# A two-layer hybrid encoder on one core: psE over strips, float32 attention, stores on GpSimd's queue, four raw buffers, and down products added to the residual in DRAM by accumulating DMAs

## The chip, the cores and the metric

One core of one Trainium2 chip runs the whole program in one launch. The metric is device time in microseconds (us); lower is better. The measured programs take the same inputs and lay the same arrays out in DRAM. Engines are named as the profile names them: PE is the matrix engine, with PEld its weight loads; DVE the vector engine, ACT the scalar engine, POOL the GpSimd engine, SP the engine whose queue issues DMAs.

## The reference

Two pre-norm residual layers over 1024 tokens of width 1024, everything in float32:

```
for layer in range(2):
    hn = rmsnorm(h, norm1_g); proj = hn @ w_in          # u 512, q 512, k 128, v 128, two gates of 1024
    y_a = s5_branch(u)      # 32 groups x 64 complex states, both directions, then gelu and a GLU
    y_b = windowed_gqa(q, k, v)   # 8 query heads, 2 key heads, width 64, window +-128, sink, relative bias
    merged = sigmoid(gate_a) * (y_a @ w_branch_a) + sigmoid(gate_b) * (y_b @ w_branch_b)
    h = h + merged @ w_out
    hn2 = rmsnorm(h, norm2_g)
    h = h + (silu(hn2 @ w_gate) * (hn2 @ w_up)) @ w_down    # inner width 2816
return rmsnorm(h, final_g)
```

Attention works on blocks of 128 queries against up to three blocks of 128 keys.

## The kernel before

Activations are kept transposed: a tile is 128 channels by 512 tokens (`HC`), and `h` runs over the two token halves. A float32 product is made of three `fp32r` products. `split` writes a rounded copy (`hi`, on ACT) and the remainder (`lo`, on DVE), and `chain` issues hi·hi, hi·lo and lo·hi for each of the k tiles of 128, so that a product over 1024 channels is 24 matmuls of 128x512. In the feed-forward part most pairs of gate and up columns are done as a `Quad`: seven products of four k tiles each (`qx`, `qy`, `qv`, `qw`) in place of eight.

Weights come in granules of up to 128x1024. `fetch` loads a granule into a `raw` buffer over SP's queue, `parts` or `quad_part` splits it (`whi` on ACT, `wlo` on DVE). There are two raw buffers and three pairs of split buffers, and `ahead` loads one granule beyond the one that is split.

The work is a list of items in a fixed order (`self.seq`), made by mixing lists by hand: projections are laid between the pieces of the state-space preparation (`s5_prep_pair`), of attention (`attention_items`) and of the state-space branch (`s5_items`). `emit` goes through the list and issues each item's instructions to the engines' queues, each of which works in order. Nearly all small tiles come from one pool `A` of `N_SLOTS` = 90 slots of 128x512 float32; PSUM has eight banks (`PS`). Every DMA, loads and stores, is issued on SP's queue (`nc.sync`).

The parts that the change touches:

- `s5_prep_pair` runs for 16 pairs of groups in each layer (layer 0: mixed with its first projections; layer 1: mixed with layer 0's feed-forward part). Its last step transposes `WB` (`pswb`) and makes, for this pair, eight small float32 products into 32 rows of `psE`: four with 112 columns (L642) and four with 16 (L644). After four pairs the bank is copied out.
- Attention: for each key head and block, `att_scores` makes for each of four heads two fp32r products over 128 rows that hold the hi and the lo part of a 64-wide query (`qe`, `qo`), with the keys' `kh` and `kl`; L793 adds the bias and takes the row maximum on DVE, ACT takes the exponential, `att_scale` divides (L810). `att_transpose` turns the probabilities and splits them (`ph`, `pl`), and `att_values` multiplies both with a value tile that holds hi and lo side by side, and adds the two halves on ACT and DVE (L832, L842).
- The state-space branch: `s5_load` reads five arrays for a pair from DRAM on SP's queue, `s5_states` makes 8 products into the two 64-row halves of a bank (`s5x`) and scans them on DVE, `s5_output` makes 12 float32 products (`s5y`), `s5_store` writes the result (`zd`).
- The feed-forward part works through groups of inner tiles (`GROUPS`). After a group's gate and up products come 16 `down` items, one for each (m, h): for a group of n tiles 3n matmuls into `dn`. Before, each item reads the residual tile from `hs` in DRAM (three items ahead), adds `dn` on DVE (L1210) and stores it back (L1212). The last group's results are kept and feed the next norm.

## Time and profile before

| | us |
|---|---|
| median of 3 runs | 2750.16 (2749.1 to 2753.0) |
| the profiled execution | 2751.03 |
| its span in the profile | 2749.2 |

Mean granted clock of PE in the profiled execution: 0.983 of full speed. The profile divides the span by engine and instruction. A busy PE is one with a matmul in flight; matmuls overlap, so what PE takes for one in a stream is read from the distance of starts in the timeline and not from the duration of one.

### The profile page before, as it was taken

The numbers are of one execution on the slowest core, as the hardware profiler recorded it, in microseconds if no ns is written. First come the engines' busy times: TensorE is split into PE (matmuls) and PEld (weight loads), VectorE is DVE, ScalarE is ACT, GpSimd is POOL, SyncE is SP. The second block draws the span as 40 slices with busy tenths as digits, with TensorE's granted clock in tenths as the row PEclk, the third lists the DMA queues.
The fourth block names the chain that finished last, engine by engine and source line by source line (L and its number), as shares of the span: only waits on it lengthen the run. The fifth ranks groups of instructions, "written<-read, shape, count | busy, mean of one in ns | idle before, by whom it ended". The sixth has DMA issues, their size and how long they took to land.

```text
span 2749.2 us, 35031 instructions
## 1 busy us (share of the span) xinstructions
PE 2651.0 (96%) x12738; PEld 2182.3 (79%) x12738; DVE 1880.3 (68%) x3881; ACT 972.1 (35%) x1829; POOL 0.2 (0%) x4
## 2 busy tenths in 40 slices
PE   8999997899999999999999999999999999999996
PEld 6788876688788888888878888888877888878775
DVE  8977988674965666656675877756377566656656
ACT  5325754432322222222345653343233223212222
POOL 0000000000000000000000000000000000000000
PEclk9999998999999999999999999999999999999998
DMA  3453235354245342553342135534415433543453
GB/s 118 133 164 112 95 113 172 120 202 139 84 125 187 105 147 73 176 169 106 123 167 75 56 108 177 177 122 154 134 65 176 162 103 131 180 161 94 138 173 132
DMA packets 205053, 367.47 MB, mean 134 GB/s; under 512 B 22304, under 2 KB 70688, under 8 KB 204880
## 3 DMA queue, kind: packets, MB, share of 16 engines
q1 hardware_dynamic: 204880, 365.23, 40.4%
q8 instruction: 100, 1.64, 0.2%
q14 instruction: 73, 0.60, 0.1%
HBM read 246.70 MB, written 118.44 MB: 133 GB/s over the span
## 4 chain that ended last, share of the span: by engine, by line
PE 80%; DVE 11%; DMA 5%; ACT 2%; issue 2%; SPq 1%; DVEq 0%; ACTq 0%
PE pj L174 6%; PE pj L175 6%; PE pj L176 6%; PE dn L174 4%; PE dn L175 4%; PE dn L176 4%; DMA raw<-in_w_up 2%; PE qy L187 2%; PE qy L185 2%; PE wo L175 2%; PE wo L174 2%; PE wo L176 2%; PE qy L186 2%; PE qv L187 2%; PE qv L186 2%; PE qv L185 2%
## 5 line engine op out<-in xcount | busy, mean ns | idle before, releaser
L162 ACT CAST whi<-raw 128x1024 fp32r<-128x1024 f32 (+3 forms) x208 | 169.5, 815 | 540.4 <-DMA raw<-in_w_down 130.8
L163 DVE TENSOR_TENSOR wlo<-raw,whi 128x1024 fp32r<-128x1024 f32 (+3 forms) x208 | 193.3, 930 | 196.7 <-ACT whi L162 188.2
L174 PE MATMUL pj<-rah,whi 128*128 128x512 f32 x768 | 308.6, 403 | 7.9 <-DVE sm L793 6.8
L175 PE MATMUL pj<-ral,whi 128*128 128x512 f32 x768 | 303.0, 395 | 3.5 <-DVE ral L112 3.5
L176 PE MATMUL pj<-rah,wlo 128*128 128x512 f32 x768 | 302.0, 394 | 0.0
L1210 DVE TENSOR_TENSOR h<-h,dn 128x512 f32<-128x512 f32 x224 | 151.0, 684 | 139.5 <-PE dn L176 98.3
L174 PEld LDWEIGHTS pj<-rah,whi 128*128 128x128 f32 x768 | 146.1, 190 | 43.3 <-DVE sm L793 8.3
L175 PEld LDWEIGHTS pj<-ral,whi 128*128 128x128 f32 x768 | 146.2, 190 | 35.0 <-DVE ral L112 6.7
L176 PEld LDWEIGHTS pj<-rah,wlo 128*128 128x128 f32 x768 | 145.8, 190 | 31.1
L185 PE MATMUL qx<-rfh,whi 128*128 128x512 f32 x256 | 100.2, 391 | 2.3 <-ACT whi L150 2.3
L187 PE MATMUL qx<-rfh,wlo 128*128 128x512 f32 x256 | 100.3, 392 | 1.0 <-DVE wlo L151 1.0
L186 PE MATMUL qx<-rfl,whi 128*128 128x512 f32 x256 | 100.1, 391 | 0.0
L174 PE MATMUL wo<-mgh,whi 128*128 128x512 f32 x256 | 100.0, 391 | 0.0
L175 PE MATMUL wo<-mgl,whi 128*128 128x512 f32 x256 | 99.7, 390 | 0.1
L176 PE MATMUL wo<-mgh,wlo 128*128 128x512 f32 x256 | 99.7, 389 | 0.0
L967 ACT COPY s5sg<-s5s 64x256 f32<-64x256 f32 x128 | 51.7, 404 | 135.1 <-DVE s5s L962 120.8
L174 PE MATMUL dn<-ffbh,whi 128*128 128x512 f32 x216 | 85.1, 394 | 0.0
L175 PE MATMUL dn<-ffbl,whi 128*128 128x512 f32 x216 | 84.2, 390 | 0.0
L175 PE MATMUL dn<-ffal,whi 128*128 128x512 f32 x216 | 84.2, 390 | 0.0
L797 ACT ACTIVATE x<-x,sm 128x384 f32<-128x384 f32 (+1 forms) x128 | 73.8, 578 | 29.3 <-DVE sm L793 29.3
L176 PE MATMUL dn<-ffah,wlo 128*128 128x512 f32 x216 | 84.1, 389 | 0.0
L174 PE MATMUL dn<-ffah,whi 128*128 128x512 f32 x216 | 84.1, 389 | 0.0
(440 smaller groups left out, 6726.3 us busy)
## 6 DMA issues: line engine op xcount, KB each, us to landing
hs<-h SPq DMA_DIRECT2D x240, 256.0 KB
h<-hs SPq DMA_DIRECT2D x240, 256.0 KB
raw<-in_w_in SPq DMA_DIRECT2D x52, 512.0 KB
raw<-in_w_gate SPq DMA_DIRECT2D x44, 512.0 KB
raw<-in_w_up SPq DMA_DIRECT2D x44, 512.0 KB
g<-th SPq DMA_DIRECT2D x64, 256.0 KB
thr<-g SPq DMA_DIRECT2D x64, 256.0 KB
raw<-in_w_down SPq DMA_DIRECT2D x80, 192.0 KB
```

What stands on the lines that cost most here:

```text
L162: nc.scalar.copy(g.hi[:, :n], g.raw[:, :n])
L163: nc.vector.tensor_tensor(g.lo[:, :n], g.raw[:, :n], g.hi[:, :n].bitcast(F32), SUB)
L174: mm(ps, lhsT=wh, rhs=xh, start=k == 0, stop=False)
L175: mm(ps, lhsT=wh, rhs=xl, start=False, stop=False)
L176: mm(ps, lhsT=wl, rhs=xh, start=False, stop=k == n - 1)
L185: mm(ps, lhsT=wh, rhs=xh, start=start and k == 0, stop=False)
L186: mm(ps, lhsT=wh, rhs=xl, start=False, stop=False)
L187: mm(ps, lhsT=wl, rhs=xh, start=False, stop=k == len(xs) - 1)
L797: nc.scalar.activation(ex[h][:, :n], ex[h][:, :n], AF.Exp, scale=-1.0, bias=nm[:, h:h + 1], accum_out=su[:, h:h + 1])
L967: nc.scalar.copy(SG[64 * r:64 * r + 64, g * 256:(g + 1) * 256].rearrange("p (d n) -> p d n", d=2), Sv[64 * g:64 * g + 64, :, r])
L1210: V.tensor_tensor(x, x, ps, ADD)
```

## The change

Six edits in one step:

1. `psE`: the eight small products of a pair are no longer issued with the pair, but for four pairs together when the fourth is there, going round the four 32-row strips with each product.
2. Attention in plain float32: queries, keys, values and probabilities are no longer split. A pair of heads lies in the two 64-row halves of the array for the scores and in its two 64-column halves for the values. The splits on DVE, the copy L832 and the sums L842 go; a copy of the probabilities on ACT, and two copies of the result on DVE for each block, stay.
3. Stores to DRAM (`sp`, `ed`, `ud`, gates, `zd`, `hs`) are issued by GpSimd's queue.
4. Four raw buffers in place of two, loads up to three granules beyond the one that is split, and 86 slots in place of 90.
5. `down` of all groups but the last: the product is copied from PSUM to a slot by ACT (`dx`), and a DMA on GpSimd's queue adds it to `hs` in DRAM. The read of `hs`, the sum on DVE and the plain store go. This concerns 5 groups in layer 0 and 7 in layer 1, 192 items.
6. Layer 1's groups are (2, 2, 3, 3, 3, 3, 3, 3) tiles in place of (2, 3, 3, 3, 3, 3, 3, 2).

```diff
@@ -24,7 +24,7 @@
 GROUPS = (((0, 5), (5, 5), (10, 3), (13, 3), (16, 3), (19, 3)),
-          ((0, 2), (2, 3), (5, 3), (8, 3), (11, 3), (14, 3), (17, 3), (20, 2)))
+          ((0, 2), (2, 2), (4, 3), (7, 3), (10, 3), (13, 3), (16, 3), (19, 3)))
 QUAD_FROM = (10, 2)
@@ -39,12 +39,13 @@
-N_SLOTS = 90
+N_SLOTS = 86
 LOOK = 2
...
 W_BUFS = 3
+R_BUFS = 4
 TB_EARLY = 4
@@ -116,10 +117,10 @@
                 i = "ab".index(g.kind)
-                r = g.quad.raw[i] = self.pw.tile([P, DM], F32, tag="raw", name="raw", bufs=2)
+                r = g.quad.raw[i] = self.pw.tile([P, DM], F32, tag="raw", name="raw", bufs=R_BUFS)
                 self.nc.sync.dma_start(r, g.quad.src[i])
             return
-        g.raw = self.pw.tile([P, DM], F32, tag="raw", name="raw", bufs=2)
+        g.raw = self.pw.tile([P, DM], F32, tag="raw", name="raw", bufs=R_BUFS)
         self.nc.sync.dma_start(g.raw[:, :g.n], g.src)
@@ -238,7 +239,7 @@
         while self.split_ < n:
-            self.fetch_to(min(self.split_ + 2, len(self.order)))
+            self.fetch_to(min(self.split_ + R_BUFS, len(self.order)))
             self.parts(self.order[self.split_])
...
@@ -628,26 +629,31 @@
         nc.scalar.copy(WBT, ps)
-        nc.sync.dma_start(sp[0], WBT)
+        nc.gpsimd.dma_start(sp[0], WBT)
...
         if i == 0:
+            self.taps = []
+        cc = [t.rearrange("p (d q h) -> p d q h", d=2, q=NPAIR)[:, :, q] for t in (p["Cr"], p["Ci"])]
+        self.taps.append((BD.rearrange("p (q d r m) -> p q d r m", q=4, d=2, r=2)[:, i],
+                          CA.rearrange("p (r d c) -> p d r c", d=2, r=2), cc))
+        if i == 3:
             self.psE = self.PS("psE")
-        BD = BD.rearrange("p (q d r m) -> p q d r m", q=4, d=2, r=2)[:, i]
-        ca = CA.rearrange("p (r d c) -> p d r c", d=2, r=2)
-        E = self.psE[32 * i:32 * i + 32]
-        cc = [t.rearrange("p (d q h) -> p d q h", d=2, q=NPAIR)[:, :, q] for t in (p["Cr"], p["Ci"])]
-        for d, dst, win in ((1, slice(0, 112), slice(16, 128)), (0, slice(128, 240), slice(0, 112))):
-            for r in range(2):
-                nc.tensor.matmul(E[:, dst], lhsT=BD[:, d, r], rhs=ca[:, d, r, win], start=r == 0, stop=r == 1)
-        for k, (d, r) in enumerate(((0, 0), (0, 1), (1, 0), (1, 1))):
-            nc.tensor.matmul(E[:, 112:128], lhsT=BD[:, d, r], rhs=cc[r][:, d], start=k == 0, stop=k == 3)
+            for d, dst, win in ((1, slice(0, 112), slice(16, 128)), (0, slice(128, 240), slice(0, 112))):
+                for r in range(2):
+                    for k, (bd, ca, _) in enumerate(self.taps):
+                        nc.tensor.matmul(self.psE[32 * k:32 * k + 32, dst], lhsT=bd[:, d, r], rhs=ca[:, d, r, win],
+                                         start=r == 0, stop=r == 1)
+            for n, (d, r) in enumerate(((0, 0), (0, 1), (1, 0), (1, 1))):
+                for k, (bd, _, cc) in enumerate(self.taps):
+                    nc.tensor.matmul(self.psE[32 * k:32 * k + 32, 112:128], lhsT=bd[:, d, r], rhs=cc[r][:, d],
+                                     start=n == 0, stop=n == 3)
         if i == 3:
...
             V.scalar_tensor_tensor(es[:, 112:128], self.m16, self.s5d[:, qq:qq + 1], es[:, 112:128], MUL, ADD)
-            nc.sync.dma_start(self.ed[l][q // 4], es[:, 0:240])
+            nc.gpsimd.dma_start(self.ed[l][q // 4], es[:, 0:240])
         yield
@@ -701,14 +707,9 @@
-        nc = self.nc
-        s = slice(64 * kv, 64 * kv + 64)
-        hh, ll = self.A(f"kh{kv}{T}", F32R), self.A(f"kl{kv}{T}", F32R)
+        kk = self.kt[kv, T] = self.A(f"kk{kv}{T}")
         for o in (slice(0, 64), slice(64, 128)):
-            nc.scalar.copy(hh[o], kn[T][s])
-        for o in (slice(0, 64), slice(64, 128)):
-            nc.vector.tensor_tensor(ll[o], kn[T][s], hh[s].bitcast(F32), SUB)
-        self.kt[kv, T] = (hh, ll)
+            self.nc.scalar.copy(kk[o], kn[T][64 * kv:64 * kv + 64])
@@ -716,16 +717,10 @@
                 nc.tensor.transpose(pt[:, b * P:(b + 1) * P], vn[T][:, b * P:(b + 1) * P], self.ident)
-            for b in range(2):
-                vt = self.A("vt", F32R)
-                o = vt.rearrange("p (k s d) -> p k s d", s=2, d=64)
-                src = pt[:, b * 256:(b + 1) * 256].rearrange("p (k d) -> p k d", d=64)
-                nc.scalar.copy(o[:, :, 0], src)
-                nc.vector.tensor_tensor(o[:, :, 1], src, o[:, :, 0].bitcast(F32), SUB)
-                self.vt.append(vt)
+            self.vt.append(self.A("vt"))
+            nc.scalar.copy(self.vt[T], pt)
     def tile_q(self, l, i, xs=None):
-        nc = self.nc
         st = {}
@@ -735,14 +730,8 @@
                 return
-            lo, up = slice(0, 64), slice(64, 128)
             for T in range(2):
-                e, o = self.A(f"qe{i}{T}", F32R), self.A(f"qo{i}{T}", F32R)
-                nc.scalar.copy(e[lo], qn[T][lo])
-                nc.vector.tensor_tensor(e[up], qn[T][lo], e[lo].bitcast(F32), SUB)
-                nc.scalar.copy(o[up], qn[T][up])
-                nc.vector.tensor_tensor(o[lo], qn[T][up], o[up].bitcast(F32), SUB)
-                self.qt[2 * i, T], self.qt[2 * i + 1, T] = e, o
+                self.qt[i, T] = qn[T]
         return self.proj(l, M_Q + i, done, xs)
...
@@ -774,25 +763,23 @@
         ex = []
-        for h in range(4):
-            hd = 4 * kv + h
-            q = self.qt[hd, Tq][:, (3 - oq) * P:(4 - oq) * P]
-            ps = self.PS("s")
-            spans = []
-            a = k0
-            while a < k1:
-                e = min(k1, (a // 4 + 1) * 4)
-                spans.append((a, e))
-                a = e
-            for w in range(2):
-                for a, e in spans:
-                    kk = self.kt[kv, a // 4][w]
-                    nc.tensor.matmul(ps[:, (a - k0) * P:(e - k0) * P], lhsT=q, rhs=kk[:, (a % 4) * P:(a % 4 + e - a) * P],
-                                     start=w == 0 and a == k0, stop=w == 1 and e == k1)
-            x = self.A("x")
-            V.tensor_tensor_reduce(out=x[:, :n], in0=ps[:, :n], in1=self.bias[hd][:, bo:bo + n], op0=ADD, op1=ALU.min,
-                                   scale=-1.0, scalar=self.nsink[:, l, hd:hd + 1], accum_out=nm[:, h:h + 1])
-            ex.append(x)
+        spans = [(a, min(k1, (a // 4 + 1) * 4)) for a in range(k0, k1) if a == k0 or a % 4 == 0]
+        for i in range(2):
+
+            pss = [self.PS("s") for _ in range(2)]
+            q = self.qt[2 * kv + i, Tq]
+            for a, e in spans:
+                for j, ps in enumerate(pss):
+                    r = slice(64 * j, 64 * j + 64)
+                    nc.tensor.matmul(ps[:, (a - k0) * P:(e - k0) * P], lhsT=q[r, (3 - oq) * P:(4 - oq) * P],
+                                     rhs=self.kt[kv, a // 4][r, (a % 4) * P:(a % 4 + e - a) * P], start=a == k0, stop=e == k1)
+            for j, ps in enumerate(pss):
+                h = 2 * i + j
+                hd = 4 * kv + h
+                x = self.A("x")
+                V.tensor_tensor_reduce(out=x[:, :n], in0=ps[:, :n], in1=self.bias[hd][:, bo:bo + n], op0=ADD, op1=ALU.min,
+                                       scale=-1.0, scalar=self.nsink[:, l, hd:hd + 1], accum_out=nm[:, h:h + 1])
+                ex.append(x)
         for h in range(4):
@@ -816,7 +803,8 @@
                 nc.tensor.transpose(ps[:, h * P:(h + 1) * P], ex[h][:, k * P:(k + 1) * P], self.ident)
-            out.append(self.split(ps, "p"))
+            out.append(self.A("p"))
+            nc.scalar.copy(out[k], ps)
         return out
@@ -825,21 +813,18 @@
             vb = k0 + k
-            v = self.vt[vb // 2][:, (vb % 2 * 2 + kv) * P:(vb % 2 * 2 + kv + 1) * P]
-            for w in range(2):
-                nc.tensor.matmul(ps, lhsT=v, rhs=pt[k][w], start=k == 0 and w == 0, stop=k == n - 1 and w == 1)
-        t = self.A("pvl")
-        nc.scalar.copy(t[0:64], ps[64:128])
+            v = self.vt[vb // 4][:, vb % 4 * P + 64 * kv:vb % 4 * P + 64 * kv + 64]
+            p = pt[k].rearrange("p (i j q) -> p j i q", i=2, j=2)
+            for j in range(2):
+
+                nc.tensor.matmul(ps[64 * j:64 * j + 64, 0:256].rearrange("p (i q) -> p i q", i=2), lhsT=v, rhs=p[:, j],
+                                 start=k == 0, stop=k == n - 1)
         T, o = divmod(b, 4)
...
                 self.yb[2 * kv + i, T] = self.A(f"yb{kv}{i}")
-        w = slice((3 - o) * P, (4 - o) * P)
-        for h in range(4):
-            y = self.yb[2 * kv + h // 2, T]
-            hp = slice(64 * (h % 2), 64 * (h % 2) + 64)
-            c = slice(h * P, (h + 1) * P)
-            nc.vector.tensor_tensor(y[hp, w], ps[0:64, c], t[0:64, c], ADD)
+        for i in range(2):
+            nc.vector.tensor_copy(self.yb[2 * kv + i, T][:, (3 - o) * P:(4 - o) * P], ps[:, i * P:(i + 1) * P])
@@ -1006,7 +991,7 @@
                               ap=[[128, 8], [1024, 16], [1, 128]])
-                nc.sync.dma_start(dst, t[:, g * 256 + k * P:g * 256 + (k + 1) * P])
+                nc.gpsimd.dma_start(dst, t[:, g * 256 + k * P:g * 256 + (k + 1) * P])
@@ -1135,7 +1120,7 @@
             V.tensor_tensor(x, x, ps, ADD)
-            nc.sync.dma_start(self.hs[m, h], x)
+            nc.gpsimd.dma_start(self.hs[m, h], x)
             if m == 0:
@@ -1198,6 +1183,14 @@
             f0, n = groups[gi]
+            if gi < last:
+
+                ps = self.PS("dn")
+                self.chain(ps, g, 0, [ff[h][f] for f in range(f0, f0 + n)])
+                t = self.A("dx")
+                nc.scalar.copy(t, ps)
+                nc.gpsimd.dma_start(self.hs[m, h], t, accum_op=ADD)
+                return
             k = orders[gi].index((m, h))
@@ -1208,14 +1201,11 @@
             V.tensor_tensor(x, x, ps, ADD)
-            if gi < last:
-                nc.sync.dma_start(self.hs[m, h], x)
-                return
             if m == 0:
...
             if l == 0:
-                nc.sync.dma_start(self.hs[m, h], x)
+                nc.gpsimd.dma_start(self.hs[m, h], x)
...
         main = []
```

## Rows read from the trace of the kernel before

**Rows 1.** The page, busy time of each engine: us (share of the span) xinstructions

```profile
PE 2651.0 (96%) x12738; PEld 2182.3 (79%) x12738; DVE 1880.3 (68%) x3881; ACT 972.1 (35%) x1829; POOL 0.2 (0%) x4
```

**Rows 2.** Windows, busy us of each engine in two stretches, PE clock, DMA

```profile
220.00:395.00 175.00, 168.48 (x943) 143.59 (x942) 152.52 (x471) 112.90 (x287) 0.00 (x0) 0.98 0.32 107
...
430.00:520.00 90.00, 73.77 (x514) 62.35 (x514) 76.78 (x162) 37.81 (x80) 0.00 (x0) 0.90 0.43 132
```

**Rows 3.** Waits of PE, whole span, last row 2640 to 2749: us, times, longest

```profile
PE s5x L939 <- DMA s5uk<-ud: 15.4, 3, 6.4
...
PE qy L185 <- ACT whi L150: 9.3, 9, 2.5
...
PE pj L174 <- DVE sm L793: 6.8, 5, 1.9
...
PE dn L174 <- ACT whi L162: 3.2, 1, 3.2
...
PE psn L301 <- DVE sqc L292: 8.9, 2, 6.1
```

**Rows 4.** PE's timeline around one s5x: start, us, line, operation, records

```profile
1740.45 0.38 PE L981 MATMUL s5y<-s5uk 128*128 128x128 f32 x2
...
1742.90 0.39 PE L984 MATMUL s5y<-s5sg,s5ca 128*128 128x127 f32 x2
1743.21 1.10 PE L939 MATMUL s5x<-s5uk,s5wbt 128*64 128x128 f32 x16
1744.24 0.50 PE L174 MATMUL pj<-rah,whi 128*128 128x512 f32 x1
1744.58 0.40 PE L175 MATMUL pj<-ral,whi 128*128 128x512 f32 x1
...
1749.59 0.39 PE L176 MATMUL pj<-rah,wlo 128*128 128x512 f32 x1
```

**Rows 5.** PE's timeline around the psE of one pair

```profile
958.41 0.95 PE L642 MATMUL psE<-CA,BD 128*32 128x112 f32 x8
959.20 0.21 PE L644 MATMUL psE<-Cr,BD 128*32 128x16 f32 x2
...
959.53 0.50 PE L174 MATMUL fu<-rfh,whi 128*128 128x512 f32 x1
959.87 0.39 PE L175 MATMUL fu<-rfl,whi 128*128 128x512 f32 x1
```

**Rows 6.** PE's timeline in layer 1's attention

```profile
1562.81 0.40 PE L830 MATMUL pv<-ph,vt 128*128 128x512 f32 x1
...
1564.20 1.03 PE L818 MATMUL pt<-cst,x 128*128 128x128 f32 x8
...
1570.53 0.33 PE L790 MATMUL s<-kh,qe 128*128 128x384 f32 x1
...
1571.94 0.39 PE L830 MATMUL pv<-ph,vt 128*128 128x512 f32 x1
```

**Rows 7.** Groups by form: shapes, count, busy us, mean ns, idle before

```profile
L1210 DVE TENSOR_TENSOR h<-h,dn 128x512 f32<-128x512 f32 x224 | 151.0, 684 | 139.5 <-PE dn L176 98.3 <-DMA h<-hs 38.5 <-issue 2.4
...
L112 DVE TENSOR_TENSOR pl<-pt,ph 128x512 fp32r<-128x512 f32 x88 | 55.5, 683 | 1.1 <-ACT ph L111 0.4
...
L810 DVE TENSOR_SCALAR x<-x,sm 128x384 f32<-128x384 f32 x96 | 35.0, 415 | 0.9
...
L810 DVE TENSOR_SCALAR x<-x,sm 128x256 f32<-128x256 f32 x32 | 9.5, 348 | 0.2
...
L1458 ACT COPY mb<-br 128x512 f32<-128x512 f32 x32 | 18.7, 583 | 8.5 <-PE br L176 8.4
```

**Rows 8.** The issuing queue of SP in layer 0's state-space stage: start, us, line, DMA, records

```profile
445.44 2.54 SPq L1009 DMA_DIRECT2D zd<-s5g  x4
...
474.01 2.53 SPq L1009 DMA_DIRECT2D zd<-s5g  x4
```

**Rows 9.** Waits of ACT, whole span: us, times, longest

```profile
ACT whi L150 <- DMA raw<-in_w_gate: 74.5, 28, 5.7
```

More of the change, by code (lines that the diff above doesn't have):

```diff
@@ L572, in s5_table_early @@
     def s5_table_early(self, l, q):
-        self.nc.sync.dma_start(self.sp[l][q][2], self.s5_table(l, q))
+        self.nc.gpsimd.dma_start(self.sp[l][q][2], self.s5_table(l, q))
     def s5_prep_pair(self, l, q):
@@ L620, in s5_prep_pair @@
             dst = bass.AP(tensor=sp[1].tensor, offset=sp[1].offset + g * 256, ap=[[HC, 64], [64 * HC, 2], [1, 256]])
-            nc.sync.dma_start(dst, CA[64 * g:64 * g + 64].rearrange("p (r c) -> p r c", r=2))
+            nc.gpsimd.dma_start(dst, CA[64 * g:64 * g + 64].rearrange("p (r c) -> p r c", r=2))
         yield
@@ L753, in done @@
             nc.scalar.copy(u, ps)
-            nc.sync.dma_start(self.ud[i][:, 4 * h:4 * h + 4, :], u.rearrange("p (j n) -> p j n", j=4))
+            nc.gpsimd.dma_start(self.ud[i][:, 4 * h:4 * h + 4, :], u.rearrange("p (j n) -> p j n", j=4))
         return self.proj(l, M_U + i, done)
@@ L763, in done @@
             store[i, h] = self.pd.tile([P, HC], F32, name=f"g{l}_{m0}_{i}_{h}")
-            nc.sync.dma_start(store[i, h], th)
+            nc.gpsimd.dma_start(store[i, h], th)
         return self.proj(l, m0 + i, done)
```

## Prediction

> **What bounds the kernel now.** I read four views in this order. The page first: PE has a matmul in flight for 2651.0 of 2749.2 us [rows 1], DVE for 1880, ACT for 972, POOL for nothing. So a microsecond taken from DVE, ACT or SP is worth something only inside the 98 us in which PE idles, and a microsecond of PE's own work is worth its full price almost everywhere. Then the windows, for the exceptions: in attention of layer 0 PE is busy 168.5 of 175 us and DVE 152.5, close behind; in the state-space stage of layer 0 the order turns, DVE 76.8 of 90 and PE 73.8 [rows 2]. Then PE's waits, which say which idle time the change can reach [rows 3]. Last the timeline, for what a matmul takes in a stream: from 1744.58 to 1749.59 lie 22 matmuls of 128x512, 0.228 us each [rows 4]. The profiled execution took 2751.0 us, 1.8 beside its span and 0.9 above the median of the runs, 2750.2; the sum below is made against 2751.0, and 0.9 is too little to change it. Under 0.2% (5.5 us) a difference can't be told from none here.
>
> **psE over strips.** A float32 product shows as two records. At full width 11 products of 128 columns (22 records) take 2.45 us, 0.111 a record; the 16 records of `s5x`, which alternate between two 64-column halves, need 1.03 us, 0.064 a record, and going into that shape and out of it costs about 0.09 (0.31 where 0.22 is due) and 0.11 (0.34 where 0.23 is due) [rows 4]. Records start in order, so the second record of one product waits for its first, while the first of the next product, on the other half, may run beside it: 16 records then take 9 times 0.111, or 1.0. That is what is seen, and I carry this rule over: n products on strips take n+1 record times in place of 2n. The eight products of a pair take 0.79 us for the four wide ones (0.099 a record) and 0.33 for the narrow ones, 1.12, and 0.11 for leaving [rows 5]: 1.23, times 32 pairs 39 us. Four pairs together: 17 records of 0.099 are 1.7, the 16 narrow ones between 0.7 and 1.3, leaving 0.1: 2.8 for 4.9, so 2.1 less, and a little more for the three entries saved: -2.25 for each of eight batches, **-18**. Both stages are bound by PE, so it counts in full. Bounds: without any overlap only three exits of 0.11 go, -3 in all; with four strips truly side by side 0.8 + 0.4 a batch, -30.
>
> **Attention in float32.** Before, scores of a block with three key blocks take 1.41 us and the values 1.39 [rows 6], for eight and six fp32r products. After: four score products of 384 columns, a record 3 times 0.111 = 0.333; two pairs on two row halves, by the same rule 5 record times, 1.67. Six value products of 256 columns, 0.222 a record, 7 record times, 1.55. That is +0.4, and two new changes of shape add 0.2: +0.6 a block, for 32 blocks (the eight with two key blocks nearly as much) **+18**. Bounds: if overlap were perfect and shapes cost nothing, 1.33 + 1.33, -5; if the row halves don't overlap, which no row shows (only column halves are in this trace), 8 times 0.333 = 2.67 for the scores, +1.0 more for each of 24 and +0.7 for each of 8 blocks, +48 in all. I take the middle because the row half is nearest to `s5x`.
>
> **DVE in attention.** The splits of the probabilities alone are 55.5 us of DVE in the two attention stages [rows 7], and the splits of keys, queries and values go with them. PE waited 6.8 us for DVE's L793 to free a bank [rows 3]: **-6**, bounds 0 and -7. The copies that stay on ACT are as long as the casts they replace.
>
> **Four raw buffers, stores off SP's queue.** ACT waits 74.5 us for gate granules to land [rows 9]; PE feels 9.3 of it at `qy` and 3.2 at `dn` [rows 3]. Loads asked for two granules earlier, with no store waiting ahead of them in SP's queue, end these: **-12**, bounds 0 and -12.5. The load still waits in SP's queue for DVE to finish with the buffer, and behind it the reads of `s5_load` and `h2`, as before.
>
> **The state-space stage of layer 0.** Each turn of the loop starts with stores of `zd` that wait for DVE and hold the next loads behind them in SP's queue; they come at 445.44 and, two turns on, at 474.01, 14.3 us a turn [rows 8]. PE waits 15.4 us in all for `s5uk` [rows 3]. With the stores on POOL the loads run ahead and DVE sets the pace: at 85% busy [rows 2] it has 12.2 us of work a turn. 2.1 us over the six turns in this window would be -13; I take **-10**, since a turn has waits of DVE for ACT that stay; bounds 0 and -15.
>
> **Layer 1's groups.** In the last group DVE adds, ACT squares, DVE sums: 2 x 0.684 us [rows 7] an item against 6 matmuls, 1.37 us, of PE, so DVE just keeps up, and PE waits 8.9 us for the sums of squares [rows 3]. With nine matmuls an item lasts 2.05: **-5**, bounds 0 and -9. PE's own work is the same.
>
> **The down products.** DVE loses 192 x 0.684 = 131 us, ACT gets 192 x 0.583 = 112 [rows 7]. PE doesn't wait for either now, so: **0**, hidden under 2.05 us of matmuls an item (1.37 in groups of two, 3.4 in groups of five). The new wait is on ACT: the copy into `dx` must wait for a free slot, which an earlier `dx` gives back only when its accumulating DMA has landed; behind that copy stand the `whi` casts of the next granules, and for those PE waits. On POOL, each accumulating store waits for its copy, and later stores queue behind; whoever reads them (the loads of the last group, `s5_load`) comes tens of us later. No row prices a store issued by POOL or an accumulation: below, it is as cheap as the plain stores on SP, four in 2.54 us [rows 8], and nothing shows; above, it is the rival below. I take nothing, for the item lasts three times a plain issue.
>
> POOL and DVE may also get in each other's way, which is one more place for a wait. L810 takes 415 ns for 384 columns and 348 for 256, 0.52 ns for one more; by that slope 512 would take 482, where L1210 takes 684 [rows 7]. So L810 runs in a faster mode than the sums. There are 128 of them, all in attention; the loop of the feed-forward part has none. The Trainium skill (SBUF — State Buffer, "SBUF: two separate sides") has a rule that speaks against the change here: while DVE runs in such a mode GpSimd can't write the descriptors of its own DMAs, and the one that comes second waits for the whole of the other. No run yet shows it. By that rule it is a rival of its own, below; in the sum it is 0, because both engines have idle time in attention.
>
> **The sum.** -18 + 18 - 6 - 12 - 10 - 5 + 0 = -33; 2751 - 33 = **2718 us**, its own range 2690 to 2740.
>
> **The rivals.**
> *Accumulating stores back up (slower).* Place: the burst of 16 down items after a group. If a store holds its slot so long that POOL and the DMA engines give back one slot each T us, and about four slots are free (my guess, from the four that the reads of `hs` held), ACT has emptied the last bank only after 12 T; PE needs 33 us for the burst. For T above 2.75 PE stops. To eat the gain, each of 12 bursts must lose 2.8 us: it decides from T = 3.0 on. At T = 3.5 a burst loses 9 us, 108 in all: 2718 + 108 = 2826. For it: no price in the trace, fewer slots (86), an addition reads DRAM where a store only writes. Against it: DMA engines are under half busy [rows 2], and the reads of the residual are gone from SP.
> *POOL and DVE block each other (slower).* If each of the 128 fast instructions had to wait for a store being issued, DVE would lose 128 times that issue: 81 us at the 0.64 of SP's [rows 8]. DVE idles 22 of 175 us in one attention stage [rows 2] and gains 28 there, twice 50, so it decides only from 0.8 us an issue on; at 1.5 us it costs 92: 2810.
> *Row halves don't overlap.* +48 for +18: 2748, no change. For it: no row with 64-row halves. Against it: the column halves overlap.
> *Strips pay in full.* psE -30 and attention -5 instead: -68, 2683. For it: four strips leave more room than the two of `s5x`; against it: `s5x` fits the rule of n+1. The Trainium skill (TensorE: Matmul & The Clock Gate, "Part 3: Packing small matmuls — row/col tiling") is on this rival's side: it has tiles start within about 4 ns of each other, and three column strips 2.38 times as fast. By that, an estimate, the 3.2 us of the 16 wide products would shrink to 1.3 and psE give -21.
> *The waits stay.* PE's waits are relabelled (a bank freed by DVE becomes one freed by ACT, the loads wait for slots): only -18 and +18 are left, 2751.
>
> **How the numbers follow.** Chances: the forecast 0.50, stores back up 0.15, POOL and DVE 0.03, no overlap on rows 0.12, full strips 0.12, waits stay 0.08. Faster by over 0.2%: 0.50 + 0.12 + half of 0.12 + about a third of 0.08 + 0.02 of the back-up (a small one) = 0.72. Within 0.2%: 0.09, from the two cases near 2750 and a mild back-up. Slower: 0.19, nearly all from the two cases with POOL. The range 2675 to 2780 takes in the full strips, no overlap and a mild back-up; 0.2 lies outside, most of it above. The likeliest is 2718.
>
> **What would show it.** Right: eight batches of `psE` at 2.6 to 3.0 us; scores near 1.7 and values near 1.55 us a block; no wait of `qy` on `whi` and none of `s5x` on `s5uk`; DVE above 90% busy in the loop at 430 us; feed-forward stretches as long as before. Wrong: PE idle inside `down` bursts with ACT waiting for `dx` or for POOL; scores of 2.7 us; POOL's stores followed by late loads of `s5uk` or `z`.

## The result and the profile after

The changed kernel takes 2665.8 us (median of 4 runs, 2663.9 to 2667.2) against 2750.8 for the kernel before on the same chip (4 runs): a ratio of 0.969 [0.9673, 0.9707], a gain of 85 us. The prediction was 2718, with a range from 2675 to 2780. The direction was right; the gain is two and a half times what I had worked out, and the time lies outside the range. The profiled execution took 2665.7 us, 1.7 beside its span of 2664.0.

The page of after, busy time of each engine, answers to [rows 1]:

```profile
PE 2597.5 (98%) x12914; PEld 2112.9 (79%) x12914; DVE 1647.1 (62%) x3481; ACT 1029.9 (39%) x1953; POOL 356.6 (13%) x524
```

PE is busy for 53 us less and idles 66 us in place of 98. DVE has lost 233 us, ACT has gained 58, and POOL is an engine with work. The windows of after show attention and the state-space stage of layer 0 as in [rows 2] (both come earlier now), and layer 1's feed-forward part from its last plain up product to its last down product. A row has start, end and length, then the busy us (and instructions) of PE, PEld, DVE, ACT and POOL, PE's granted clock, the DMA share and GB/s:

```profile
205.00:375.00 170.00, 169.49 (x1045) 127.41 (x1043) 108.70 (x387) 100.14 (x268) 18.99 (x33) 1.00 0.33 110
405.00:490.00 85.00, 67.97 (x495) 57.49 (x495) 73.13 (x158) 33.76 (x73) 11.96 (x20) 0.90 0.44 139
2018.00:2645.00 627.00, 624.34 (x2752) 513.93 (x2751) 349.14 (x527) 239.36 (x407) 96.45 (x112) 1.00 0.49 108
```

In attention PE idles for 0.5 of 170 us, and DVE, close behind it before, is busy 64% of the time. In the state-space stage DVE still leads, at 86%, no more than before. In the feed-forward part PE is idle for 2.7 of 627 us, at a granted clock of 1.00. The same stretch of before, by its windows:

```profile
2069.00:2728.00 659.00, 638.58 (x2754) 518.65 (x2752) 417.74 (x635) 178.79 (x292) 0.00 (x0) 0.98 0.44 147
```

With as many matmuls (2754 and 2752) PE was idle for 20.4 us here, and busy for 14 us longer, at a mean granted clock of 0.98. So a stretch of 659 us is now one of 627: by its first and last starts, 658.3 and 627.3, it is 31 us shorter. The forecast had given it a part of the 12 us of the raw buffers and the 5 of the groups.

PE's waits of after, whole span (us, times, longest), stand against [rows 3]:

```profile
PE s5x L924 <- DMA s5uk<-ud: 11.5, 1, 11.5
PE pj L175 <- ACT xgh L361: 7.0, 1, 7.0
...
PE s5x L924 <- DVE s5a L935: 5.5, 1, 5.5
PE psn L302 <- DVE sqc L293: 5.2, 2, 3.1
...
PE s5x L924 <- DVE sm L780: 1.0, 2, 0.5
```

No wait on `whi` is left at `qy` or `dn`, and none for the freed bank of the scores. The wait for `s5uk` is now a single one of 11.5 us, late in the state-space loop of layer 0 (it ends at 465.9 us). All waits at `s5x` together are 18.0 us; before they were 18.1, in three rows (15.4, 1.8 and 0.9). Of the prediction's signs of being right, one was seen, `qy` without a wait on `whi`; the batches of `psE` (1.3 us), the scores (1.49), the values (1.44), DVE in the loop, the wait of `s5x` and the length of the feed-forward part all came out otherwise.

### The profile page after: what moved, and what is told of

Read it like the earlier page. It is cut to its first block, busy times and chain, and to the rows that moved or that the text cites. A ratio compares the mean times of both kernels' runs of the same rounds, so it can differ in the third digit from the quotient of the medians.

```text
span 2664.0 us, 35136 instructions
## 1 busy us (share of the span) xinstructions
PE 2597.5 (98%) x12914; PEld 2112.9 (79%) x12914; DVE 1647.1 (62%) x3481; ACT 1029.9 (39%) x1953; POOL 356.6 (13%) x524
## 4 chain that ended last, share of the span: by engine, by line
PE 87%; DVE 7%; DMA 2%; ACT 2%; issue 1%; SPq 0%; POOL 0%; DVEq 0%; ACTq 0%; POOLq 0%
PE pj L175 6%; PE pj L176 6%; PE pj L177 6%; PE dn L175 6%; PE dn L176 6%; PE dn L177 6%; PE wo L175 2%; PE wo L176 2%; PE wo L177 2%; PE qv L186 2%; PE qy L186 2%; PE qv L187 2%; PE qy L187 2%; PE qv L188 2%; PE qy L188 2%; PE qx L186 2%
## 5 line engine op out<-in xcount | busy, mean ns | idle before, releaser
L1192 POOL DMA_DIRECT2D hs<-dx x192 | 165.7, 864 | 818.6 <-ACT dx L1191 710.5
L1191 ACT COPY dx<-dn 128x512 f32<-128x512 f32 x192 | 111.9, 584 | 86.4 <-PE dn L177 80.4
L780 DVE CUSTOM_DVE_ANT_0 x<-s,bias,nsink 128x384 f32<-128x384 f32 (+1 forms) x128 | 67.8, 581 | 89.4 <-PE s L774 88.8
L112 ACT CAST ffah<-ts 128x512 fp32r<-128x512 f32 x32 | 19.9, 622 | 176.5 <-DVE ts L1274 176.5
```

The lines of the kernel that those rows point to most:

```text
L780: V.tensor_tensor_reduce(out=x[:, :n], in0=ps[:, :n], in1=self.bias[hd][:, bo:bo + n], op0=ADD, op1=ALU.min, scale=-1.0, scalar=self.nsink ...
L1191: nc.scalar.copy(t, ps)
L1192: nc.gpsimd.dma_start(self.hs[m, h], t, accum_op=ADD)
```

## The experiments

Each kernel was timed beside runs of the kernel before on its own chip. "Worth" is the distance of its ratio from the 0.969 of after, or from 1 for a kernel built on before, times 2750.8 us; with intervals of about ±0.0018 on each ratio it is good to some 5 to 7 us. Two kernels more, read by their timelines, have one run each (2707.9 and 2667.9 us) and stand below.

| kernel | us | ratio to before | worth |
|---|---|---|---|
| after, psE per pair again | 2697.2 | 0.9801 [0.9784, 0.9818] | +31 |
| after, two raw buffers | 2697.4 | 0.9800 [0.9778, 0.9822] | +30 |
| after, three raw buffers | 2675.9 | 0.9722 [0.9706, 0.9738] | +9 |
| after, six raw buffers | 2668.4 | 0.9694 [0.9678, 0.9711] | +1 |
| after, four buffers, two loads ahead | 2667.3 | 0.9692 [0.9678, 0.9707] | +1 |
| after, plain stores on SP | 2666.3 | 0.9689 [0.9671, 0.9708] | 0 |
| after, no accumulating DMA | 2680.4 | 0.9738 [0.9720, 0.9756] | +13 |
| the same, residual read on GpSimd's queue | 2691.8 | 0.9794 [0.9775, 0.9813] | +29 |
| after, DVE copies the down products | 2670.4 | 0.9717 [0.9702, 0.9733] | +7 |
| after, layer 1's groups of before | 2676.2 | 0.9729 [0.9713, 0.9744] | +11 |
| before, float32 attention | 2737.1 | 0.9959 [0.9940, 0.9977] | -11 |
| before, four raw buffers | 2725.5 | 0.9904 [0.9886, 0.9922] | -26 |
| before, stores on GpSimd's queue | 2735.4 | 0.9949 [0.9931, 0.9967] | -14 |

### What a strip costs

**psE per pair.** The strips are undone, all else stays:

```diff
-        if i == 3:
-            ...                                  # four pairs together, strip by strip
+        for d, dst, win in ((1, slice(0, 112), slice(16, 128)), (0, slice(128, 240), slice(0, 112))):
+            for r in range(2):
+                nc.tensor.matmul(E[:, dst], lhsT=BD[:, d, r], rhs=ca[:, d, r, win], start=r == 0, stop=r == 1)
+        ...
```

> The changed kernel with psE again made pair by pair, all else as changed. Theory (strips run fully side by side): in the changed kernel the 32 wide and 32 narrow records of a batch take 1.18 us and 0.11 for leaving the shape, against 4 x 1.23 in the kernel before, so 3.6 us come back in each of 8 batches: 2666 + 29 = 2695 us. Rival (n products on strips take n+1 record times, the rule of the prediction): 2666 + 18 = 2684 us.

Measured: +31. The price of "n+1 records" would have been +18, the price of strips that run fully side by side +29 to +30. The timeline of after shows the same thing in one batch (start, us, line, operation, records):

```profile
920.39 0.97 PE L645 MATMUL psE<-CA,BD 128*32 128x112 f32 x32
921.18 0.23 PE L649 MATMUL psE<-Cr,BD 128*32 128x16 f32 x8
...
921.57 0.50 PE L175 MATMUL fu<-rfh,whi 128*128 128x512 f32 x1
921.91 0.39 PE L176 MATMUL fu<-rfl,whi 128*128 128x512 f32 x1
```

From start to start the 32 wide records take 0.79 us. That is what the 8 records of a single pair took before [rows 5]: four pairs in the time of one. With 0.39 for the narrow ones and the 0.11 for leaving the shape (0.34 where 0.23 is due) the batch costs 1.29 where four pairs cost 4.92, -3.6 for each of eight batches, -29. The Trainium skill (TensorE: Matmul & The Clock Gate, "Part 3: Packing small matmuls — row/col tiling") has tiles that start within about 4 ns of each other; the trace nearly agrees, with starts some 7 ns apart within a round of four, and 0.79 us for 32 records against 0.79 for 8. The section's 2.38 for three strips, from which the prediction's estimate of -21 was worked out, falls short of full overlap; the trace shows full overlap on four.

**Float32 attention alone**, in the kernel before: only the functions from `key_tiles` to `att_values` are taken from after.

> The kernel before with float32 attention alone. Theory (strips fully side by side, each stretch pays a fixed tail of about 0.17 us): PE's work in attention grows by 0.2 to 0.3 us a block, +8 us, and the waits for DVE's L793 go, -10: 2747 to 2751 us, no difference. Rival (n+1 record times): +18 - 6, 2763 us. Rival (the time won by DVE matters beyond those waits): below 2740 us.

Measured: -11, and not the +18 - 6 of the rule and the waits.

**The score products twice**, in the kernel after, puts the rule to the test by itself. Each pair of products is issued a second time into the same bank; in a block with its keys in one tile, as below, this begins the sum anew (it doesn't add to the first, as the expectation has it):

```diff
-            for a, e in spans:
+            for a, e in spans * 2:
```

> The changed kernel with the score products of every block issued twice, the second pass of a span adding to the first (so the scores are wrong, and only the length of the stretch is read). One block with three key blocks took 1.49 us from the first score to the first value product. Theory (records of two strips fully side by side, 0.32 us for a record of 384 columns, plus a fixed tail of 0.17 for the stretch): 8 x 0.32 + 0.17 to 0.21 = 2.73 to 2.77 us. Rival (n+1 record times of 0.333): 9 x 0.333 = 3.0 us. Rival (no fixed part, all scales): 2.98 us.

The timeline of after, one block of three key blocks:

```profile
1561.29 1.56 PE L774 MATMUL s<-kk,qn 64*128 64x384 f32 x8
1562.78 1.52 PE L820 MATMUL pv<-p,vt 128*64 128x256 f32 x12
1564.22 1.53 PE L805 MATMUL pt<-cst,x 128*128 128x128 f32 x12
```

And of the kernel with the products twice:

```profile
1598.55 2.85 PE L774 MATMUL s<-kk,qn 64*128 64x384 f32 x16
1601.34 1.52 PE L820 MATMUL pv<-p,vt 128*64 128x256 f32 x12
```

From start to start: scores 1.49, values 1.44, doubled scores 2.79. A record of 384 columns is 0.333 (3 times 0.111, [rows 4]). Eight of them on two halves, fully side by side, are 1.33, sixteen 2.67, and twelve value records of 0.222 are 1.33. What is left is 0.16, 0.12 and 0.11: one fixed cost for a stretch, whatever its length. `s5x` fits too: 16 records of 0.111 on two halves are 0.89, and 0.14 are left of its 1.03 [rows 4]. This is the row on which I had built n+1, and it can't tell the two laws apart, since there the one more record (0.11) and the fixed cost (0.14) are nearly alike.

**The row halves not alternated.** In blocks where the keys span two tiles each head's two products are issued one behind the other:

```diff
-            for a, e in spans:
-                for j, ps in enumerate(pss):
+            for j, ps in enumerate(pss):
+                for a, e in spans:
```

> The changed kernel with the scores' products of one row half issued before those of the other where a block's keys lie in two spans (blocks 3 and 4 of each head), all other blocks as they are. Theory: records run side by side only with the record next in order, so where the two spans of one half follow each other the overlap shrinks: a two-span block's scores go from 1.51 us to about 1.8. Rival: the array takes records of the other half from further behind, then they stay at 1.5 us.

In the timeline of that kernel a two-span block, and the same block in after:

```profile
1552.57 1.68 PE L774 MATMUL s<-kk,qn 64*128 64x128 f32 x16
1554.18 1.52 PE L820 MATMUL pv<-p,vt 128*64 128x256 f32 x12
```

```profile
1551.39 1.58 PE L774 MATMUL s<-kk,qn 64*128 64x128 f32 x16
1552.90 1.52 PE L820 MATMUL pv<-p,vt 128*64 128x256 f32 x12
```

1.61 us, against 1.51 in after. It lies between the two expectations: most of the overlap survives when the halves aren't alternated product by product.

### What two more raw buffers give

**Two, three and six buffers** in the kernel after (`R_BUFS`; the slots stay at 86 for two and three, and go to 82 for six), **four buffers with loads issued two ahead**, and **four buffers in the kernel before**:

```diff
-            self.fetch_to(min(self.split_ + R_BUFS, len(self.order)))
+            self.fetch_to(min(self.split_ + 2, len(self.order)))       # four buffers, two loads ahead
```

> The changed kernel with two raw buffers and loads one granule ahead. Theory: the four buffers ended PE's waits for granules in the feed-forward part (quad products took 22 us less, down products 11 less); with two they come back, about +25: 2690 us, and PE waits for whi at qy again. Rival: the waits ended because stores no longer stand before loads in SP's queue; then two buffers are enough and the time stays at 2666, at most 2670.

> The kernel after with three raw buffers in place of four (and 86 slots as they are). My theory: what the two further buffers gave (31 us, 2697 with two of them) is the landing time of a weight load, which with two buffers lies between the moment DVE lets a buffer go and the cast that needs it; one further buffer already puts a whole granule's work (some 10 us of PE) between the two, so most of the gain is there: 2666 to 2674. Rival, that the gain comes from evening out longer hold-ups of SP's queue, each worth several granules: half of it stays away, 2678 to 2686.

> The kernel after with six raw buffers, paid with four slots (82 in place of 86). My theory: ACT no longer waits for weights to land in the kernel after, so further buffers find nothing to save: 2662 to 2668, no difference. Rival (hold-ups of several granules are left, as the waits of s5x and pj suggest): 2652 to 2660. Rival (slots are short): 2675 and above, with PE waits on a free slot in attention or in the down bursts.

> The kernel after with four raw buffers, but loads are again issued only two granules ahead of the split, as before. It tells the two halves of the edit apart: the buffers and the order in SP's queue. My theory: the load issued two ahead finds its buffer free at once instead of waiting for DVE, so half to all of the gain is kept: 2666 to 2680. Rival (the place of the issue in SP's queue is what counts): as with two buffers, 2690 to 2697.

> The kernel before with four raw buffers, issued four ahead, and 86 slots; all else as before (stores on SP's queue, reads of the residual, split attention). My theory: the gain of the buffers, 31 us when it is undone in the kernel after, is there without the other parts: 2718 to 2726. Rival (SP's queue, with its stores and residual reads that wait for DVE, holds the loads back however many buffers there are): 2738 to 2750. My prediction's term of 12 us, if it had been right in its size: 2739.

Measured: +30, +9, +1, +1, and -26 in the kernel before (its feed-forward part of layer 1 takes 637.6 us in place of 658.3, by the same starts). So the gain is that of the buffers themselves, not of the place of a load in SP's queue; it is there without the other edits; the third buffer brings about two thirds of it, a little less than I expected, and the fifth and sixth nothing.

Where it comes from is to be read on ACT, not on PE. ACT's waits in the kernel before, one row more than [rows 9]:

```profile
ACT whi L162 <- DMA raw<-in_w_down: 130.8, 28, 7.7
```

The largest such row in the kernel before with four buffers, and below it the one in after:

```profile
ACT whi L151 <- DMA raw<-in_w_gate: 16.6, 8, 6.0
```

```profile
ACT whi L163 <- DMA raw<-in_w_in: 8.6, 5, 3.3
```

Before, ACT waited 205 us for weights in two rows (130.8 here and 74.5 in [rows 9]), in 56 waits. In PE's own list only 12.5 of that carried the name of `whi` in [rows 3], and 2.3 more in a row for `qx`.

ACT's total says where to look, not how much there is to gain: in after with two buffers ACT waits 92 us for weights, less than half of the 205, and the two buffers are worth as much (30 us there, 26 in the kernel before).

The timeline of the kernel with two buffers shows what becomes of such a wait:

```profile
2115.67 0.33 SPq L121 DMA_DIRECT2D raw<-in_w_gate  x1
...
2122.66 1.05 ACT L151 CAST whi<-raw 128x1024 fp32r<-128x1024 f32 x1 [4.39 <-DMA raw<-in_w_gate]
...
2123.74 1.23 DVE L152 TENSOR_TENSOR wlo<-raw,whi 128x1024 fp32r<-128x1024 f32 x1 [5.14 <-ACT whi L151]
...
2127.51 0.68 DVE L1259 TENSOR_TENSOR qu<-qp,qy 128x512 f32<-128x512 f32 x1
...
2122.69 0.39 PE L188 MATMUL qx<-rfh,wlo 128*128 128x512 f32 x1
2128.25 0.79 PE L186 MATMUL qy<-tt2h,whs 128*128 128x512 f32 x1 [5.17 <-DVE qu L1259]
2128.84 0.63 PE L187 MATMUL qy<-tt2l,whs 128*128 128x512 f32 x1
2129.27 0.63 PE L188 MATMUL qy<-tt2h,wls 128*128 128x512 f32 x1
```

A load asked for at 2115.67 is there for the cast at 2122.66. ACT has waited 4.4 us for it, DVE's split waits 5.1 for the cast, and DVE's `qu`, which reads a bank that PE needs, stands in DVE's order behind the split and the sums of the granule that came after it. PE idles 5.2 us, and its list calls it a wait for `qu`; the weight is not named. Nor is that all: up to 2134.39 the next 13 matmuls start 0.43 us apart in place of 0.23, and the window of 5 us from 2128 has a granted clock of 0.50, the 1.2 GHz level, where 5 us before the gap had 1.00, the level of 2.4 GHz:

```profile
2128.00:2133.00 5.00, 4.75 (x11) 3.79 (x12) 3.82 (x6) 1.65 (x4) 0.00 (x0) 0.50 0.32 105
2118.00:2123.00 5.00, 5.00 (x23) 3.87 (x21) 0.60 (x1) 0.61 (x2) 1.17 (x2) 1.00 0.96 240
```

One late weight cost a gap that was put down to DVE, and 13 matmuls at about half speed, 2.6 us.

### SP's queue and the stores

**The plain stores back on SP**, in after (the accumulating DMAs stay on POOL):

```diff
-            nc.gpsimd.dma_start(...)        # sp, ed, ud, gates, zd, hs
+            nc.sync.dma_start(...)
```

> The changed kernel with all plain stores back on SP's queue; only the accumulating DMAs stay on POOL. Theory: with four raw buffers a load may stand behind a store for a while without harm, so only the state-space loop of layer 0 suffers, where the loads of a pair wait behind the stores of zd: +5 to +10, 2671 to 2676 us. Rival: the stores were what held the granules back, then +25 and PE waits for whi at qy: 2690 us.

**The stores on GpSimd's queue, in before**: the same edit the other way, the residual's stores too.

> The kernel before with all its plain stores, those of the residual too, issued by GpSimd's queue in place of SP's; two raw buffers as before. In the kernel after, the same stores put back on SP changed nothing (2666.3). My prediction had 10 us of the state-space stage and part of 12 us of weight loads on this move. Theory: with two buffers a load has no slack, so a store that waits ahead of it in SP's queue does cost, and the loop of the state-space stage of layer 0 gets shorter: 2735 to 2745. Rival (the loads wait for DVE to let a buffer go, whatever stands ahead in the queue): no difference, 2747 to 2754.

Measured: 0 with four buffers, -14 with two. The +5 to +10 that I expected of the first of these runs don't show. The second run shows what the move is worth with two buffers, where a store that waits for DVE stands ahead of a load that has no slack; with four buffers no such cost shows. ACT's waits in the second kernel, in the two rows that were 130.8 and 74.5 us:

```profile
ACT whi L150 <- DMA raw<-in_w_gate: 42.6, 19, 4.6
ACT whi L162 <- DMA raw<-in_w_down: 30.7, 12, 4.5
```

Stores and buffers thus remove the same waits. From the first `s5x` to the first `glu` (starts in the timelines) layer 0's state-space stage takes 157.6 us before, 151.7 with the stores moved, 148.4 in after and 151.0 in after with the stores on SP. The last blocks of attention lie in this stretch too, though, and with float32 attention alone, stores on SP, it already is 151.4. From the first `br` on, the branch product that comes behind these blocks, the four are 112.7, 109.7, 108.4 and 111.1: about 3 us of the 10 I gave it come with the move, with two buffers and with four. In a total that is good to 7 us they can't be seen.

Why no more, SP's queue itself shows. Its longest waits in this stage, before (430 to 520 us) and below it in after (400 to 490):

```profile
SPq L1009 <- DVE s5g L1004: 39.6, 6, 15.2
```

```profile
SPq L124 <- DVE wlo L164: 33.9, 2, 18.6
```

Where the stores of `zd` held the queue, a weight load now does: it waits until DVE's split gives a raw buffer back, and the loads of the next pair stand behind it. The `s5uk` for which PE waits 11.5 us is issued 1.9 us after this load:

```profile
458.63 0.34 SPq L124 DMA_DIRECT2D raw<-in_w_br_a  x1
...
460.49 0.38 SPq L904 DMA_DIRECT2D s5uk<-ud  x1
```

### The down products

**No accumulating DMA**: the items of the first groups read the residual on SP's queue, DVE adds, and POOL stores, as before. **The same with the reads on GpSimd's queue**, and **accumulating, but copied by DVE**:

```diff
-                nc.scalar.copy(t, ps)
+                nc.vector.tensor_copy(t, ps)               # third kernel only
                 nc.gpsimd.dma_start(self.hs[m, h], t, accum_op=ADD)
```

> The changed kernel with down products read, added by DVE and stored as in the kernel before (reads on SP, stores on POOL). Theory: nothing that PE waits for hangs on it, 2666 to 2670 us, with DVE 131 us busier and ACT 112 less. Rival: DVE's sums and SP's reads delayed the splits of the next granules, then +10 to +20 with waits of PE in the feed-forward part: 2676 to 2686 us.

> The kernel after without accumulating DMAs (DVE adds each down product to the residual, as before, and POOL stores the sum), where GpSimd's queue issues the reads of the residual as well. With the reads on SP's queue it took 2680.4, 14.6 more than after. Theory 1, that DVE's 192 additions (131 us) are what costs, because DVE splits the weights in the same stages: it stays, 2677 to 2684. Theory 2, that the reads of the residual wait in SP's queue for buffers and hold the weight loads behind them: the cost goes, 2664 to 2670.

> The kernel after with accumulating DMAs, but DVE and not ACT copies each down product from its bank (192 copies of 128x512). There are no reads of the residual at all. Theory 1 (DVE's time is what the accumulating DMAs save): DVE has again some 100 to 131 us more, and most of the 14.6 us comes back: 2674 to 2682. Theory 2 (the reads in SP's queue): 2664 to 2669.

Measured: +13, +29 and +7. My theory of "nothing" falls. About half of the 13 comes back when DVE does the copies and there are no reads. So about half goes with DVE's time; that the rest belongs to the reads, since DVE can't add before the residual has landed, is argued and not shown by itself. The reads on GpSimd's queue stand behind stores that wait for DVE, and it gets worse. DVE's waits for the residual in that kernel, to be held against 15.1 us with the reads on SP and 1.7 in after:

```profile
DVE h L1195 <- DMA h<-hs: 65.4, 44, 3.9
```

How the 13 divide can't be read closer than the intervals allow. In the feed-forward part of layer 1, from the same first to the same last start, the kernel without accumulation needs 641.8 us against 627.3: this is where nearly all of its loss lies.

What the accumulating DMA costs, by the page of after (groups: busy us, mean ns; issue: KB, median us to landing):

```profile
L1192 POOL DMA_DIRECT2D hs<-dx x192 | 165.7, 864 | 818.6 <-ACT dx L1191 710.5
...
L1191 ACT COPY dx<-dn 128x512 f32<-128x512 f32 x192 | 111.9, 584 | 86.4 <-PE dn L177 80.4
...
hs<-dx POOLq DMA_DIRECT2D x192, 256.0 KB, 5.8
...
hs<-h POOLq DMA_DIRECT2D x48, 256.0 KB, 2.3
```

0.86 us of POOL an item, against an item of 1.4 us or more; POOL is the one that waits, 710 us of it for ACT's copy. That copy waits for PE's product (80 of 86 us); no wait for a slot shows.

**Layer 1's groups** as before:

```diff
-          ((0, 2), (2, 2), (4, 3), (7, 3), (10, 3), (13, 3), (16, 3), (19, 3)))
+          ((0, 2), (2, 3), (5, 3), (8, 3), (11, 3), (14, 3), (17, 3), (20, 2)))
```

> The changed kernel with layer 1's groups as before: (2, 3, 3, 3, 3, 3, 3, 2) tiles. Theory: the last group of two lets DVE fall behind the down products, PE waits for the sums of squares again, +4 to +6: 2670 to 2672 us. Rival: the tail is set by the last norm whatever the group's size: within 2 us of 2666.

Measured: +11; direction as expected, size about twice. PE's waits for the sums of squares in that kernel:

```profile
PE psn L302 <- DVE sqc L293: 9.3, 3, 5.5
```

4.1 of the 11 are this wait. Another 3 to 4 are PE's clock behind it. After a wait of 1.9 us for `sqc` that after doesn't have, 14 matmuls of the last group, on both sides of a wait for `rs` of 2.5, start 0.34 to 0.57 us apart, most of them 0.43. In after the same matmuls run at the full clock, though the wait for `rs` is there as well. A window of each kernel, that without the edit first:

```profile
2638.00:2640.00 2.00, 2.00 (x6) 1.41 (x5) 1.17 (x5) 0.00 (x0) 0.00 (x0) 0.50 0.00 0
```

```profile
2636.00:2640.00 4.00, 4.00 (x19) 3.29 (x18) 4.00 (x7) 0.63 (x1) 0.00 (x0) 1.00 0.64 230
```

By the starts in the timeline `dn` takes 500 us against 494; these waits and slow matmuls lie in it. The rest of the 11 is within the intervals.

## Why the prediction was wrong

By its own terms, against what the runs give when a part is undone or done alone:

| term | predicted | measured |
|---|---|---|
| psE over strips | -18 | -31 |
| attention in float32, with DVE's waits | +18 - 6 | -11 (by the timelines +1 of PE's products, -11 of waits and what is behind them) |
| raw buffers, and stores off SP's queue | -12 | -26 to -30 by the buffers, -14 by the stores, which overlap |
| state-space stage of layer 0 | -10 | 4 us shorter behind attention's last blocks, 3 of them by the stores; 0 in the total |
| layer 1's groups | -5 | -11 |
| down products | 0 | -13 |

**n+1 records on strips is the step that failed most by its size**: it carried two terms, -18 and +18, and PE's products gave about -30 and +1, 30 of the 52 us that the forecast is off. It was a law drawn from one row that two laws fit. The rival "strips pay in full" named the other, at a chance of 0.12, and had its psE right (-30 for -31). For attention it gave -5 from PE's own work; by the starts in the timelines the scores and values of all 32 blocks now take 87.1 us where they took 85.9. A block of three key blocks goes from 2.80 [rows 6] to 2.93, but the scores of the eight with two spans from about 1.82 to 1.51. The gain of 11 comes from around them: the transpositions and what stands behind them fall from 50.9 to 39.9 us. In these lie PE's waits for DVE, and PE's list before does name them, in two rows that I left out beside the 6.8 us of L793 in [rows 3]:

```profile
PE pt L818 <- DVE sm L793: 3.3, 2, 2.0
...
PE s5x L939 <- ACT th L762: 1.8, 2, 0.9
```

Of these 11.9 us after has 1.0 left, at `s5x`. So the -6 was too small because one row of three was read. That rival's 2683 was still 17 above the result.

**The raw buffers** failed next. I bounded the gain by the 12.5 us of PE's waits that carry the name of `whi`, and called it a bound. It isn't one: 26 to 30 came. PE's list names the last link before PE, and a late weight reaches PE through ACT's cast, DVE's split and whatever stands behind these two in their orders; and PE comes back at half its clock. ACT's 74.5 us stood in [rows 9], in the sum they only served to explain PE's 9.3. The bound from above that the trace allowed was the 98 us in which PE idled, with what the clock lost behind its gaps; ACT's 205 us told where to look.

**The down products at nothing** failed on the same point as the buffers: 131 us of DVE and the reads of the residual were no wait of PE by name, but DVE splits the weights in the same stages. The feared side was wrong as well. The accumulating stores don't back up: POOL needs 0.86 us an item, and in the burst of a group of two tiles from 2020 us on, where items come fastest, the 16 stores land 2.0 us apart on average, so T is under the 2.75 us from which PE would have stopped. Nor do POOL and DVE block each other in a way that shows. The groups of DVE after have

```profile
L797 DVE TENSOR_SCALAR x<-x,sm 128x384 f32<-128x384 f32 x96 | 33.8, 417 | 0.8
```

where the same instruction (L810 then) took 415 ns with POOL idle [rows 7]. Of all 128 of them 24 ran while POOL issued a store; none took over 443 ns, and these issues took 0.54 to 0.73 us. The rule of the Trainium skill (SBUF — State Buffer, "SBUF: two separate sides") changes nothing that can be measured here.

**The state-space stage** failed in its mechanism. I had the stores of `zd` as what holds the loads, and the waits for `s5uk` gone with them; DVE is at 86% and not over 90%, and PE waits as long at `s5x` as before (18.0 us for 18.1). A weight load now holds SP's queue ahead of the longest of these waits, 11.5 us; no run took it away, so what it costs by itself is not shown. Behind attention's last blocks the stage is 4 us shorter, 3 of which go with the stores. **The groups** had the mechanism right (the wait for `sqc` is 9.3 without the edit and 5.2 with it) and half the size, for want of the clock behind the wait.

Undone or done one at a time, the parts add up to about 96 (31 + 11 + 30 + 0 + 13 + 11), and the whole is 85. With 5 to 7 us on each part the two don't contradict each other; that waits which two edits remove are counted twice, as those of stores and buffers are, would go the same way.

## What to carry to other kernels

A bound engine's list of waits names the last link only: before a wait is taken as the bound of a gain, look at the waits of the engines that feed it, and at the clock behind each gap. Take all rows of the list that one cause can stand behind: attention's waits had three names. And when a queue is cleared of one hold-up, look which comes next in it. Where a row fits two laws, keep both prices and weigh the choice as a risk of its own, above all when it carries two terms of the sum. Buffers ahead of a tight chain are worth trying in number: here the third and fourth gave a third of the whole gain, and two more none.

## What the hardware showed

- Float32 products on two or four strips ran fully side by side: psE's wide records took 0.79 us for one pair on one strip or four on four; scores 1.49 and 2.79 us for 8 and 16 records of 384 columns on two row halves. Stretches on two halves had 0.11 to 0.16 us more as a whole.
- After a gap of 5.2 us PE came back at a granted clock of 0.50, and 13 matmuls started 0.43 us apart.
- An accumulating DMA of 256 KB from GpSimd's queue took 0.86 us to issue and landed after 5.8 us in the median; a plain store of a residual tile of the same size took 0.55 and landed after 2.3.
